# An encoder step on one core: four places where a low part, or the order of two input tiles, changes

## The chip, the core and the metric

The kernel runs on one core of one Trainium2 chip. The metric is the time of one execution on the device, in microseconds (us). The core has five engines that run their own instruction streams and wait for each other through semaphores: TensorE (PE in the profile; its weight loads are PEld), VectorE (DVE), ScalarE (ACT), GpSimd (POOL) and SyncE (SP). SP and POOL issue nearly all of the transfers here.

## The reference

One layer of a streaming encoder over 576 tokens (512 of a prompt and 64 of a running stream), model width 1024, feed-forward width 2816, all in float32:

```
x += 0.5 * SwiGLU_1(RMSNorm(x))
h  = RMSNorm(x); p = h @ w_in                       # 1024 x 7168
y_a = (B_a * dwconv3(C_a * V_a)) @ w_a_out
y_b = swish(LN(dwconv31(GLU(U_b)) + bias)) @ w_b_out
x += (sigmoid(g_a) * y_a + sigmoid(g_b) * y_b) @ w_out
x += 0.5 * SwiGLU_2(RMSNorm(x))
y  = RMSNorm(x)
```

SwiGLU is `(silu(x @ gate) * (x @ up)) @ down`. The outputs are y and the last input rows of the two convolutions.

## The kernel before, in words

Activations lie with features on the 128 partitions and the 576 tokens along the free dimension, so each of the 8 tiles of x is 128x576. Every product is made of matmuls of a 128x128 weight tile with half of the tokens (288 columns).

**Three matmuls for one.** A float32 operand v is split in two parts, hi (v rounded to TensorE's fast float32 form) and lo = v - hi. A product is the sum of hi·hi, hi·lo and lo·hi, and `SIX` lists those three for the two token halves: six matmuls for each weight tile and input tile (line 55 on). The first four entries use the weight's hi, the last two its lo.

**Making a weight's two parts.** The class `Stream` brings weights in: SP loads a raw tile (`load`), ACT rounds it to hi (`begin`), and lo is made in one of two ways. With `"dma"`, ACT writes -hi into the place of lo, and then a transfer that POOL issues adds the raw tile to it. With `"dve"`, VectorE subtracts hi from the raw tile (`end`). There are six raw tiles; a raw tile is free again when the last reader of it is done, which is the adding transfer in the first way and the subtraction in the second. The weights come in units of up to four 128x128 tiles, in an order fixed by a plan that is written before the program; `get` hands out a unit, and `lead` starts units some places ahead. The lo parts (and hi) live in the tiles called `u`, `g` or `act`.

**Products.** `product` makes one output tile (8 input tiles, 48 matmuls where both halves have 4 weight tiles). With `late`, its last two input tiles are taken in turn by `turned`: hi matmuls of the one, all six of the other, then the lo matmuls of the first. `both` makes two output tiles side by side. Where the layout allows, two weight tiles are multiplied by a scheme with seven products of 12 matmuls instead of eight (`plan_block`, `pair`, `block_pair`); its seven weight operands are three plain blocks (a11, a12, a22, which take the way given by `low`) and four sums.

**The stages that the change touches.**
- The head: while x and the first weights still arrive, `multiply(k)` feeds three products (up 0, gate 0, gate 1 of the first feed-forward) with input tile k, k from 0 to 7; `begin(k)` makes the two parts of x's tile k, `split_piece` those of the weights. Then comes the product ("f1", "u", 1), inside of which the total for RMSNorm is formed (`root`).
- The w_out stage: after the last scheme of seven products of w_b_out (`block_pair(3)`), `both` starts the output tiles 0 and 4 of w_out (`IN_TURN` is 0, 4, 1, 5, ...), each of two units.
- The second feed-forward: tile 0 goes by plain products (`PLAIN["f2"]` is 1), tiles 1, 2, ... by `pair`, seven products each.

Instructions go to each engine in the order in which this program is written; nothing is reordered afterwards.

Of the kernel before, what the change touches and what calls it, by code (L numbers as in the profile page):

```python
# [15 lines left out]
P = 128  # L16
D = 1024
KT = D // P
# [4 lines left out]
KU = KT // 2  # L23
# [30 lines left out]
PLAIN = {"f1": 4, "f2": 1}  # L54

IN_TURN = (0, 4, 1, 5, 2, 6, 3, 7)


SIX = ((0, 0), (1, 0), (0, 1), (1, 1), (2, 0), (2, 1))


SHIFT = 32
# [49 lines left out]
def tile_encoder_step(  # L112
# [7 lines left out]
    pe, dve, sca, pool = (  # L120
        Ordered(tc, e, c)
        for e, c in (
            (nc.tensor, pe_cost), (nc.vector, dve_cost), (nc.scalar, None), (nc.gpsimd, None)
        )
    )
# [33 lines left out]
    def psum2():  # L159
        return mmps.tile([P, 2, 512], F32, tag="mm", name=nm("mm"))  # L160
# [161 lines left out]
    homes = [0]  # L322

    def home(other):

        homes[0] += 1
        return ("u", other)[homes[0] % 2]

    def plan_tile(name, w, row0, ks, col0, other, home_of=None, low="dma"):
        plan[name] = []  # L330
        for k in ks:
            r = ws.raw(w, row0, k, col0)
            to = next(home_of) if isinstance(home_of, Iterator) else home_of or home(other)
            plan[name].append(ws.unit(r, k, to, low))
            row0 += k * P

    FIRST = [("f1", "u", 0), ("f1", "g", 0), ("f1", "g", 1)]

    def gu_col(part, i):
        return i * P + (DFF if part == "u" else 0)  # L340

    def plan_pair(f, gu, i):

        plan_block((f, "s", i), [
            ws.raw(gu, h * KU * P, KU, gu_col(part, i)) for part in "ug" for h in range(2)
        ], [home("g") for _ in range(7)], "dve" if (f, i) == ("f1", PLAIN[f]) else "dma")

    def plan_block(name, raws, homes, low="dma"):  # L350

        a21, a22, a11, a12 = raws
        s1, s2, s3, s4 = ((name, n) for n in range(1, 5))
        plan[name] = [
            ws.unit(src, KU, home, how, sums)
            for home, (src, how, sums) in zip(homes, (
                (a11, low, ((s1, (a21, a22)),)),
                (s2, "dve", ((s2, (s1, a11)),)),
                (s1, "dve", ()),
                (s3, "dve", ((s3, (a11, a21)),)),  # L360
                (a12, low, ()),
                (s4, "dve", ((s4, (s2, a12)),)),
                (a22, low, ()),
            ))
        ]
        ws.second.update(plan[name][n] for n in (1, 5, 6))

    def plan_ffn(f, gu, dn):
        for g, grp in enumerate(GROUPS):
            for i in grp:  # L370
                if i >= PLAIN[f]:
                    plan_pair(f, gu, i)
                    continue
                for part in "gu":
                    if (f, part, i) not in plan:
                        plan_tile(
                            (f, part, i), gu, 0, (KU, KU), gu_col(part, i), "g",
                            low="dve" if f == "f1" and (part, i) != ("u", 1) else "dma",
                        )
            n = len(grp)  # L380
            for j in range(KT):
                late = f == "f2" and grp[-1] == FT - 1 and j in LATE
                soon = (f, g) == ("f1", 0) and j < 2 or late and j >= KT - 2
                plan_tile(
                    (f, "d", g, j), dn, grp[0] * P, (n - n // 2, n // 2), j * P, "g",
                    "act" if late else None, "dve" if soon else "dma",
                )
# [27 lines left out]
    for i in range(KU):  # L415
        pair = 2 * i, 2 * i + 1
        if i % 2 == 0:
            for j in pair:

                plan_mixer(("yb", j), w_b_out, j * P, homes_b, "dve")  # L420
        else:

            plan_block(("yb", "s", i), [
                ws.raw(w_b_out, h * P, KU, j * P, 2) for j in pair[::-1] for h in range(2)
            ], [next(homes_b) for _ in range(7)])
    for j in IN_TURN:
        plan_tile(("o", j), w_out, 0, (KU, KU), j * P, "g")
    plan_ffn("f2", ffn2_gu, ffn2_dn)


    def mm(ps, w, kk, xs, first, last, spans=HALVES, six=SIX):


        (whi, wlo), (xh, xl) = w, xs
        parts = ((whi, xh), (whi, xl), (wlo, xh))
        for n, s in six:
            if s < len(spans):
                (a, b), (i, e) = parts[n], spans[s]
                pe.matmul(
                    ps[:, s, : e - i], a[:, kk, :], b[:, i:e],  # L440
                    start=first and n == 0, stop=last and n == 2,
                )

    def chunks(name):

        got = []
        for n in plan[name]:
            w = ws.get(n)
            got += [(w, kk) for kk in range(ws.units[n][1])]
        return got  # L450
# [15 lines left out]
    def fill():  # L466
        while work and dve.time < pe.time - AHEAD:
            work.pop(0)()

    def take():  # L470

        while behind:
            ready, then = behind.pop(0)
            dve.time = max(dve.time, ready)
            then()
# [5 lines left out]
    def turned(p, w, kk, xs, k, last):  # L481

        mm(p, w, kk, xs[k], k == 0, False, six=SIX[:4])
        mm(p, w, kk + 1, xs[k + 1], False, False)
        mm(p, w, kk, xs[k], False, last, six=SIX[4:])

    def product(name, xs, then=None, order=None, got=None, soon=None, late=False):


        if name in early:  # L490
            return early.pop(name)[:, :, :H]
        ps = psum2()
        if order:
            got = chunks(name)
            for n, k in enumerate(order):
                mm(ps, *got[k], xs[k], n == 0, n == len(xs) - 1)
        else:
            at = {0} if turning[0] else set()
            if late:
                at.add(len(xs) - 2)  # L500
            turning[0] = False
            k = 0
            for n in plan[name]:
                w = None
                if not got:
                    w = ws.get(n)
                end = k + ws.units[n][1]
                k0 = k
                while k < end:
                    w = got[k][0] if got else w  # L510
                    if k in at:
                        turned(ps, w, k - k0, xs, k, k + 2 == len(xs))
                        k += 2
                        continue
                    mm(ps, w, k - k0, xs[k], k == 0, k == len(xs) - 1)
                    k += 1
                    if soon and k == 1:
                        soon()
        take()
        if then is None:  # L520
            dve.time = max(dve.time, pe.time)
            return ps[:, :, :H]
        fill()
        behind.append((pe.time, lambda: then(ps[:, :, :H])))

    def both(names, xs, turn=False):
# [4 lines left out]
        for k in range(len(xs)):  # L531
            if turn and k == 1:
                for n, six in (0, SIX[:4]), (1, SIX), (0, SIX[4:]):
                    mm(ps[n], *ws_[n][k], xs[k], False, False, six=six)
# [168 lines left out]
    xg = []  # L703
# [37 lines left out]
    def piece_of(k):  # L741

        for n, size in enumerate(FIRST_KS):
            if k < size:
                return n, k
            k -= size

    first = {name: psum2() for name in FIRST}

    def multiply(k, names=FIRST):  # L750
        n, kk = piece_of(k)
        up, gates = pieces[n][2]

        for six in (SIX,) if k > 0 else (((0, 0), (2, 0), (0, 1), (2, 1)), ((1, 0), (1, 1))):
            for name, (hi, lo), c in zip(FIRST, (up, gates, gates), (0, 0, P)):
                if name in names:
                    w = hi[:, :, c : c + P], lo[:, :, c : c + P]
                    mm(first[name], w, kk, xg[k], k == 0, k == KT - 1, six=six)

    load(0)  # L760
    load_piece(FIRST_KS[0], (nc.sync, sca))
# [15 lines left out]
    begin(1)  # L777
    split_piece(1, sca)
    multiply(0)
    begin(2)  # L780
    split_piece(2, sca)
    multiply(1)
    ss.square(X[0])
    begin(3)
    ss.square(X[1])
    multiply(2)
    begin(4)
    ss.add(dve)
# [36 lines left out]

    ws.ahead = 2
    name = ("f1", "u", 1)
    ps = product(name, xg, soon=root)
    early[name] = ps

    def update(j, ps, R=None):
# [149 lines left out]
    ss, xg = nss, nxg  # L981
# [69 lines left out]
    gates = {}  # L1051
# [32 lines left out]
    xg = xn  # L1084
# [223 lines left out]
    xg = [None] * KT  # L1308
    forms = Forms(R_N2)
    ss = Sum()  # L1310
    xg = [None] * KT
# [3 lines left out]
    for n, j in enumerate(IN_TURN):  # L1315
        ps = two[j] if j in two else product(("o", j), MS)
# [146 lines left out]
```

## Time and profile before

| | |
|---|---|
| median of 3 runs | 1287.59 us (1286.79, 1287.59, 1296.06) |
| the profiled execution | 1297.4 us, its span 1295.4 us |
| PE busy | 1284.4 us (99%), 9728 matmuls |
| DVE, ACT, POOL busy | 924.8, 764.6, 361.1 us (71%, 59%, 28%) |
| granted TensorE clock | 0.998 of full speed, mean |
| transfers issued by POOL | 56160 packets, 92.43 MB, 43.3% of the 16 DMA engines' span |
| transfers issued by SP and ACT | 228784 and 1744 packets, 120.35 and 0.83 MB |

All operations of the compute engines carry one line number (88 before, 92 after), that of a helper that records them, so the trace is read by the names of tiles. Rows of the timeline give the start, the time from the first start to the last end of the rows merged into one, the engine, the operation with its tiles, the count, and in brackets how long the engine had been idle and what ended that. Ends of matmuls are modelled; their starts are recorded, so the steps here go by starts.

### The profile page before, as it was taken

How to read it: one execution, taken by the hardware profiler on the slowest of the kernel's cores; microseconds unless marked ns; L12 is line 12 of the kernel's file. 1: busy time of each engine (PE TensorE's matmuls, PEld its weight loads, DVE VectorE, ACT ScalarE, POOL GpSimd, SP SyncE). 2: the span in 40 equal slices, each digit the busy share in tenths (PEclk: the TensorE clock that was granted, in tenths of full speed). 3: DMA queues.
4: the chain of work that ended last, by engine and by line, in shares of the span. 5: the costliest groups of instructions: out<-in, count | busy, mean ns of one | idle time of the engine just before them, and what ended most of it. 6: DMA issues, size and time to landing. Idle time of an engine off the chain costs nothing.

```text
span 1295.4 us, 25702 instructions
## 1 busy us (share of the span) xinstructions
PE 1284.4 (99%) x9728; PEld 1282.8 (99%) x9728; DVE 924.8 (71%) x1539; ACT 764.6 (59%) x1359; POOL 361.1 (28%) x460
## 2 busy tenths in 40 slices
PE   9999999999999999999999999999999999999997
PEld 9999999999999999999999999999999999999997
DVE  6858668748846998888885166746867858846955
ACT  7645646646776644554444566468664665664664
POOL 0032332332333444333321221132142241241230
PEclk9999999999999999999999999999999999999999
DMA  8286786886799898878875766597588797796783
GB/s 221 69 180 153 163 179 154 179 177 150 153 223 230 177 199 164 169 166 175 168 167 125 165 137 157 143 238 157 124 170 180 159 191 156 161 199 142 154 180 96
DMA packets 286812, 215.26 MB, mean 166 GB/s; under 512 B 15456, under 2 KB 248928, under 8 KB 286688
## 3 DMA queue, kind: packets, MB, share of 16 engines
q0 software_dynamic: 56160, 92.43, 43.3%
q1 hardware_dynamic: 228784, 120.35, 32.5%
q8 instruction: 77, 1.26, 0.4%
q10 hardware_dynamic: 1744, 0.83, 0.2%
q14 instruction: 47, 0.39, 0.1%
HBM read 116.17 MB, written 4.98 MB: 94 GB/s over the span
## 4 chain that ended last, share of the span: by engine, by line
PE 92%; issue 4%; DVE 2%; DMA 1%; ACT 1%; POOL 0%; DVEq 0%; SPq 0%; POOLq 0%; ACTq 0%
PE mm L88 92%; DVE tmp L88 0%; DMA g<-raw 0%; DMA raw<-in_w_b_out_dram 0%; DVE x L88 0%; DMA u<-raw 0%; DVE g L88 0%; ACT act L88 0%; DMA raw<-in_ffn_w_gate_up_dram 0%; DVE act L88 0%; DVE w L88 0%; POOL u L88 0%; ACT u L88 0%; ACT w L88 0%; ACT g L88 0%
## 5 line engine op out<-in xcount | busy, mean ns | idle before, releaser
L88 PE MATMUL mm<-act,u 128*128 128x288 f32 x4758 | 670.8, 294 | 0.5 <-DMA u<-raw 0.5
L88 PEld LDWEIGHTS mm<-act,u 128*128 128x128 f32 x4758 | 641.6, 188 | 0.7 <-DMA u<-raw 0.7
L88 PE MATMUL mm<-act,g 128*128 128x288 f32 x3030 | 432.9, 294 | 0.8 <-DMA g<-raw 0.8
L88 PEld LDWEIGHTS mm<-act,g 128*128 128x128 f32 x3030 | 410.4, 188 | 1.0 <-DMA g<-raw 1.0
L88 POOL DMA_DIRECT2D u<-raw x197 | 171.9, 873 | 487.7 <-ACT u L88 318.8
L88 PE MATMUL mm<-act,act 128*128 128x288 f32 (+2 forms) x1896 | 262.1, 295 | 0.0
L88 PEld LDWEIGHTS mm<-act,act 128*128 128x128 f32 x1896 | 254.5, 189 | 0.3 <-ACT act L88 0.3
L88 ACT CAST u<-raw 128x512 fp32r<-128x512 f32 (+2 forms) x207 | 118.8, 574 | 178.4 <-PE mm L88 145.3
L88 POOL DMA_DIRECT2D g<-raw x126 | 110.0, 873 | 298.4 <-ACT g L88 247.3
L88 DVE SCALAR_TENSOR_TENSOR w<-g,prm,w 128x606 f32<-128x606 f32 x232 | 179.2, 842 | 1.4 <-ACT w L88 1.4
L88 DVE TENSOR_TENSOR tmp<-mm,tmp 128x288 f32<-128x288 f32 (+1 forms) x251 | 112.6, 458 | 71.7 <-PE mm L88 54.9
L88 ACT ACTIVATE u<-u 128x512 fp32r<-128x512 f32 (+2 forms) x197 | 116.8, 593 | 6.2
L88 ACT CAST g<-raw 128x512 fp32r<-128x512 f32 (+2 forms) x136 | 75.1, 552 | 43.0 <-PE mm L88 21.0
L88 DVE SCALAR_TENSOR_TENSOR tmp<-mm,r 128x576 f32<-128x576 f32 x48 | 36.3, 756 | 76.7 <-PE mm L88 76.7
L88 POOL DMA_DIRECT2D act<-raw x67 | 59.2, 883 | 108.9 <-ACT act L88 95.0
L88 ACT CAST act<-tmp 128x576 fp32r<-128x576 f32 x92 | 61.8, 674 | 42.4 <-DVE tmp L88 40.9
L88 ACT CAST u<-w 128x512 fp32r<-128x512 f32 x81 | 50.2, 620 | 62.0 <-DVE w L88 44.1
L88 ACT CAST g<-w 128x512 fp32r<-128x512 f32 x79 | 48.9, 619 | 63.4 <-DVE w L88 56.4
L88 DVE TENSOR_TENSOR act<-tmp,act 128x576 fp32r<-128x576 f32 x92 | 67.5, 753 | 18.1 <-ACT act L88 16.5
L88 ACT ACTIVATE g<-g 128x512 fp32r<-128x512 f32 (+2 forms) x126 | 72.1, 572 | 4.0
L88 DVE TENSOR_TENSOR w<-raw,raw 128x512 f32<-128x512 f32 x82 | 56.1, 685 | 15.1 <-DMA raw<-in_ffn_w_gate_up_dram 11.1
L88 ACT ACTIVATE tmp<-tmp 128x576 f32<-128x576 f32 x47 | 32.2, 685 | 45.9 <-DVE tmp L88 45.9
(86 smaller groups left out, 829.3 us busy)
## 6 DMA issues: line engine op xcount, KB each, us to landing
raw<-in_ffn_w_gate_up_dram SPq DMA_DIRECT2D x171, 256.0 KB, 3.5
u<-raw POOLq DMA_DIRECT2D x140, 256.0 KB, 4.0
raw<-in_w_in_dram SPq DMA_DIRECT2D x112, 256.0 KB, 3.7
raw<-in_ffn_w_down_dram SPq DMA_DIRECT2D x96, 192.0 KB, 3.7
g<-raw POOLq DMA_DIRECT2D x69, 256.0 KB, 4.0
act<-raw POOLq DMA_DIRECT2D x61, 256.0 KB, 4.4
g<-raw POOLq DMA_DIRECT2D x43, 192.0 KB, 4.4
u<-raw POOLq DMA_DIRECT2D x41, 192.0 KB, 4.6
```

Of the source, the lines that this page charges most:

```text
L88: return self.tc.keep_in_program_order(fn(*args, **kwargs))
```

## The change

Four places:
- `multiply(6)` no longer runs its three products one after the other with six matmuls each: the up product does its four hi matmuls, gate 0 its six, up its two lo matmuls, gate 1 its six.
- the product ("f1", "u", 1) is called with `late=True`.
- the lo parts of w_out's first four units (output tiles 0 and 4) are made by VectorE instead of by a transfer.
- in the second scheme of seven products of the second feed-forward (tile 2), the lo part of a22, the last of the seven weight operands, is made by VectorE.

```diff
+FIRST_SIX = (((0, 0), (2, 0), (0, 1), (2, 1)), ((1, 0), (1, 1)))
+
+HEAD_TURN = 6
...
-        ], [home("g") for _ in range(7)], "dve" if (f, i) == ("f1", PLAIN[f]) else "dma")
-
-    def plan_block(name, raws, homes, low="dma"):
+        ], [home("g") for _ in range(7)], {
+            ("f1", PLAIN["f1"]): ("dve", "dve", "dve"), ("f2", PLAIN["f2"] + 1): ("dma", "dma", "dve"),
+        }.get((f, i), ("dma", "dma", "dma")))
+
+    def plan_block(name, raws, homes, lows=("dma", "dma", "dma")):
...
     for j in IN_TURN:
-        plan_tile(("o", j), w_out, 0, (KU, KU), j * P, "g")
+        plan_tile(
+            ("o", j), w_out, 0, (KU, KU), j * P, "g",
+            low="dve" if j in IN_TURN[:2] else "dma",
+        )
...
-    def multiply(k, names=FIRST):
+    def multiply(k):
...
+        steps = [(n, SIX) for n in range(len(FIRST))]
+        if k == 0:
+            steps = [(n, six) for six in FIRST_SIX for n in range(len(FIRST))]
+        elif k == HEAD_TURN:
+            steps = [(0, SIX[:4]), (1, SIX), (0, SIX[4:]), (2, SIX)]
+        for n, six in steps:
+            (hi, lo), c = ((up, 0), (gates, 0), (gates, P))[n]
+            w = hi[:, :, c : c + P], lo[:, :, c : c + P]
+            mm(first[FIRST[n]], w, kk, xg[k], k == 0, k == KT - 1, six=six)
...
-    ps = product(name, xg, soon=root)
+    ps = product(name, xg, soon=root, late=True)
```

On VectorE, around the start of the w_out stage, the order before is this. The `act<-w` row and the two `act<-x` rows make lo parts; the rows with `mm` are sums of the seven products.

```order
L88 TENSOR_TENSOR act_10398<-w_10367,act_10397 128x512
L88 TENSOR_TENSOR tmp_10430<-mm_10444,tmp_10430 128x288
L88 TENSOR_TENSOR tmp_10431<-mm_10483,tmp_10430 128x288 x2
L88 TENSOR_TENSOR tmp_10429<-tmp_10431,mm_10483 128x288
L88 TENSOR_TENSOR act_10540<-x_94,act_10538 128x576
L88 TENSOR_TENSOR act_10544<-x_95,act_10542 128x576
L88 TENSOR_TENSOR tmp_10428<-mm_10523,tmp_10430 128x288
```

Now the same place reads as follows.

```order
L92 TENSOR_TENSOR act_10398<-w_10367,act_10397 128x512
L92 TENSOR_TENSOR g_10458<-raw_10229,g_10457 128x512
L92 TENSOR_TENSOR tmp_10430<-mm_10444,tmp_10430 128x288
L92 TENSOR_TENSOR u_10476<-raw_10252,u_10476 128x512
L92 TENSOR_TENSOR tmp_10431<-mm_10478,tmp_10430 128x288
L92 TENSOR_TENSOR g_10496<-raw_10307,g_10495 128x512
L92 TENSOR_TENSOR tmp_10431<-mm_10478,tmp_10430 128x288
L92 TENSOR_TENSOR tmp_10429<-tmp_10431,mm_10478 128x288
L92 TENSOR_TENSOR act_10533<-x_94,act_10531 128x576
L92 TENSOR_TENSOR act_10537<-x_95,act_10535 128x576
L92 TENSOR_TENSOR u_10514<-raw_10438,u_10514 128x512
L92 TENSOR_TENSOR tmp_10428<-mm_10516,tmp_10430 128x288
```

Four subtractions of a raw tile (into `g` and `u`, the four units of w_out) have come in between the sums. Four steps of ACT that wrote -hi and four transfers of POOL are gone from their engines' streams.

On VectorE, in the second scheme of the second feed-forward, the rows before are these.

```order
L88 TENSOR_TENSOR w_11529<-raw_11386,raw_11388 128x512
L88 TENSOR_TENSOR tmp_11375<-mm_11508,tmp_11373 128x288
L88 TENSOR_TENSOR w_11554<-w_11529,raw_11449 128x512
L88 TENSOR_TENSOR tmp_11375<-tmp_11375,tmp_11374 128x576
L88 TENSOR_TENSOR tmp_11524<-mm_11561,tmp_11524 128x288
```

Now they are these.

```order
L92 TENSOR_TENSOR w_11525<-raw_11382,raw_11384 128x512
L92 TENSOR_TENSOR tmp_11371<-mm_11504,tmp_11369 128x288
L92 TENSOR_TENSOR u_11527<-raw_11097,u_11527 128x512
L92 TENSOR_TENSOR w_11549<-w_11525,raw_11445 128x512
L92 TENSOR_TENSOR tmp_11371<-tmp_11371,tmp_11370 128x576
L92 TENSOR_TENSOR tmp_11520<-mm_11556,tmp_11520 128x288
```

One subtraction (`u<-raw`, a22's lo) has come in behind the last sum of the scheme before it.

On PE, in the head, input tile 6 (`act_297` and `act_298` are its hi and lo; 302 and 303 those of the up weights, 306 and 307 those of the two gates) reads so before.

```order
L88 MATMUL mm_108<-act_297,act_302 128x288
L88 MATMUL mm_108<-act_298,act_302 128x288
L88 MATMUL mm_108<-act_297,act_302 128x288
L88 MATMUL mm_108<-act_298,act_302 128x288
L88 MATMUL mm_108<-act_297,act_303 128x288 x2
L88 MATMUL mm_109<-act_297,act_306 128x288
L88 MATMUL mm_109<-act_298,act_306 128x288
L88 MATMUL mm_109<-act_297,act_306 128x288
L88 MATMUL mm_109<-act_298,act_306 128x288
L88 MATMUL mm_109<-act_297,act_307 128x288 x2
```

Now it reads so.

```order
L92 MATMUL mm_108<-act_297,act_302 128x288
L92 MATMUL mm_108<-act_298,act_302 128x288
L92 MATMUL mm_108<-act_297,act_302 128x288
L92 MATMUL mm_108<-act_298,act_302 128x288
L92 MATMUL mm_109<-act_297,act_306 128x288
L92 MATMUL mm_109<-act_298,act_306 128x288
L92 MATMUL mm_109<-act_297,act_306 128x288
L92 MATMUL mm_109<-act_298,act_306 128x288
L92 MATMUL mm_109<-act_297,act_307 128x288 x2
L92 MATMUL mm_108<-act_297,act_303 128x288 x2
```

The two matmuls with the up weights' lo have moved from the fifth and sixth place to the eleventh and twelfth; their number is the same.

More of the change, by code (lines that the diff above doesn't have):

```diff
@@ L356, in plan_block @@
             for home, (src, how, sums) in zip(homes, (
-                (a11, low, ((s1, (a21, a22)),)),
+                (a11, lows[0], ((s1, (a21, a22)),)),
                 (s2, "dve", ((s2, (s1, a11)),)),
@@ L360, in plan_block @@
                 (s3, "dve", ((s3, (a11, a21)),)),
-                (a12, low, ()),
+                (a12, lows[1], ()),
                 (s4, "dve", ((s4, (s2, a12)),)),
-                (a22, low, ()),
+                (a22, lows[2], ()),
             ))
@@ L748, in tile_encoder_step @@
     first = {name: psum2() for name in FIRST}
-    def multiply(k, names=FIRST):
+    def multiply(k):
         n, kk = piece_of(k)
         up, gates = pieces[n][2]
[L754 to L758, printed above, removed]
+        steps = [(n, SIX) for n in range(len(FIRST))]
[7 more added lines that the diff above has]
+            mm(first[FIRST[n]], w, kk, xg[k], k == 0, k == KT - 1, six=six)
     load(0)
```

## The prediction

> **What bounds the kernel now.** I read the page first, then PE's waits, then PE's timeline where a wait stands, then the engines that feed PE there. On the page:
>
> ```profile
> span 1295.4 us, 25702 instructions
> PE 1284.4 (99%) x9728; PEld 1282.8 (99%) x9728; DVE 924.8 (71%) x1539; ACT 764.6 (59%) x1359; POOL 361.1 (28%) x460
> ```
>
> PE runs nearly without a break, so only its number of matmuls, their pitch, and its few waits set the end. The change keeps the number. The waits of PE for transfers, in all (engine, whom it waited for, total us, times, longest):
>
> ```profile
> PE mm L88 <- DMA g<-raw: 0.8, 1, 0.8
> PE mm L88 <- DMA u<-raw: 0.5, 1, 0.5
> ```
>
> Each happened once. The bracketed figures use modelled ends; I size the two losses by starts. PE around the w_out stage (start, length, operation, count; two answers of the timeline):
>
> ```profile
> 832.28 3.32 PE L88 MATMUL mm<-act,u 128*128 128x288 f32 x24
> 835.44 3.33 PE L88 MATMUL mm<-act,g 128*128 128x288 f32 x24
> 838.61 1.74 PE L88 MATMUL mm<-act,u 128*128 128x288 f32 x12
> ```
>
> ```profile
> 848.11 3.10 PE L88 MATMUL mm<-act,g 128*128 128x288 f32 x22
> 851.99 5.27 PE L88 MATMUL mm<-act,g 128*128 128x288 f32 x38 [0.77 <-DMA g<-raw]
> 857.10 6.48 PE L88 MATMUL mm<-act,u 128*128 128x288 f32 x48
> ```
>
> Undisturbed, 24 matmuls take 835.44 - 832.28 = 3.16 us, a pitch of 0.1317. From 848.11 to 857.10 there are 22 + 38 = 60 matmuls, 7.90 us at that pitch, in 8.99: **1.09 us lost**. The row of 22 is 12 of the last product of `block_pair(3)` and 10 of the w_out stage: six of output tile 0, four with the hi of tile 4's first unit. What is waited for is that unit's lo.
>
> PE in the second feed-forward:
>
> ```profile
> 925.52 1.75 PE L88 MATMUL mm<-act,u 128*128 128x288 f32 x12
> ...
> 933.45 1.75 PE L88 MATMUL mm<-act,g 128*128 128x288 f32 x12
> 935.03 0.43 PE L88 MATMUL mm<-act,u 128*128 128x288 f32 x2
> 935.92 1.58 PE L88 MATMUL mm<-act,u 128*128 128x288 f32 x10 [0.46 <-DMA u<-raw]
> 937.34 1.75 PE L88 MATMUL mm<-act,g 128*128 128x288 f32 x12
> ```
>
> A product of 12 takes 935.03 - 933.45 = 1.58 us; the one from 935.03 took 2.31: **0.73 us lost**. A scheme is seven products; the one that begins at 925.52 is the second, and its seventh, a22's, is the one that waits.
>
> **The w_out units.** Who is late there (ACT, then DVE, then POOL):
>
> ```profile
> 845.01 0.62 ACT L88 CAST g<-raw 128x512 fp32r<-128x512 f32 x1 [1.45 <-PE mm L88]
> ```
>
> ```profile
> 845.14 0.82 DVE L88 TENSOR_TENSOR tmp<-mm,tmp 128x288 f32<-128x288 f32 x2 [2.28 <-PE mm L88]
> 848.06 1.43 DVE L88 TENSOR_TENSOR act<-x,act 128x576 fp32r<-128x576 f32 x2 [1.61 <-ACT act L88]
> ```
>
> ```profile
> 846.59 0.86 POOL L88 DMA_DIRECT2D g<-raw  x1 [1.88 <-ACT g L88]
> ```
>
> The same transfer's group of issues (KB each, us to landing):
>
> ```profile
> g<-raw POOLq DMA_DIRECT2D x1, 256.0 KB, 5.4
> ```
>
> Hi ends at 845.63, the adding transfer is issued at 846.59 and lands 5.4 us later, at 851.99, when PE goes on. After the change VectorE subtracts as soon as hi is there. I price a subtraction by its nearest row, a DVE subtraction of the same shape:
>
> ```profile
> 837.36 0.69 DVE L88 TENSOR_TENSOR g<-w,g 128x512 fp32r<-128x512 f32 x1
> ```
>
> So this lo is ready near 845.63 + 0.69 = 846.3, four and a half us before PE asks (848.11 + 22 x 0.132 = 851.0). The wait goes whole: **-1.09**. The four subtractions, 2.8 us, fall into DVE's idle 2.28 and 1.61 us, and the four ACT steps and four POOL issues that go free those engines. Behind the subtraction that waits for hi stand on DVE the second sum of the row at 845.14 (from about 845.6 to 846.3), a difference and the two lo parts of x (848.06 before, bound by ACT, which is now earlier). PE needs those two from input tile 4, 48 matmuls into the stage, about 856: cover of over 6 us. If that cover were gone, each subtraction would cost its 0.69. A raw tile that comes free sooner lets SP load sooner; see the last rival.
>
> **The a22 unit.** ACT, DVE, and POOL with the issue groups of its transfers:
>
> ```profile
> 929.58 0.60 ACT L88 CAST u<-raw 128x512 fp32r<-128x512 f32 x1
> 930.22 0.63 ACT L88 ACTIVATE u<-u 128x512 fp32r<-128x512 f32 x1
> ```
>
> ```profile
> 930.08 0.45 DVE L88 TENSOR_TENSOR tmp<-mm,tmp 128x288 f32<-128x288 f32 x1
> 930.45 0.68 DVE L88 TENSOR_TENSOR w<-w,raw 128x512 f32<-128x512 f32 x1
> 932.34 0.46 DVE L88 TENSOR_TENSOR tmp<-mm,tmp 128x288 f32<-128x288 f32 x1 [0.55 <-ACT tmp L88]
> ```
>
> ```profile
> 921.84 0.86 POOL L88 DMA_DIRECT2D u<-raw  x1 [4.18 <-ACT tmp L88]
> ...
> 931.81 0.86 POOL L88 DMA_DIRECT2D u<-raw  x1 [4.36 <-ACT g L88]
> 932.35 1.21 POOL L88 DMA_DIRECT2D g<-raw  x1
> ...
> 942.79 0.86 POOL L88 DMA_DIRECT2D u<-raw  x1 [0.32 <-ACT tmp L88]
> ```
>
> ```profile
> u<-raw POOLq DMA_DIRECT2D x1, 256.0 KB, 4.1
> g<-raw POOLq DMA_DIRECT2D x1, 256.0 KB, 4.8
> ```
>
> The wait is on 931.81 + 4.1 = 935.9. VectorE would have this lo at 930.53 + 0.69 = 931.2. **-0.73.** On DVE the added 0.69 pushes w (930.45) and what follows; the idle 0.55 takes most of it. The weight sum that is pushed (930.45) feeds the next scheme's second product, after 938.9: cover of 6 us. ACT saves 0.63 us just before the next unit's hi.
>
> **What is late next.** PE comes 1.09 earlier to all that lies behind 852, and 1.82 earlier behind 936. Up to the second wait the feeding chain starts from the w_out products themselves, so it moves along: the u transfer of 921.84, landing 3.5 us on (row below) at 925.34, is needed by the third matmul at 925.52 + 0.26 = 925.78 and keeps its 0.44. Behind the second wait the 0.73 is not shared by all of the chain. The g transfer of 932.35 lands at 937.15 and is needed at 937.60: 0.45 to spare. It gains the 0.63 of ACT and a queue without its predecessor, so I take it as just enough. The u transfer of 942.79 is similar:
>
> ```profile
> u<-raw POOLq DMA_DIRECT2D x1, 256.0 KB, 3.5
> ```
>
> ```profile
> 948.44 1.75 PE L88 MATMUL mm<-act,u 128*128 128x288 f32 x12
> ```
>
> ```profile
> u<-raw POOLq DMA_DIRECT2D x1, 256.0 KB, 4.9
> ```
>
> Landing 947.69, needed 948.70: 1.0 to spare, less 0.73, less up to 0.3 by which DVE is later. New waits here lie between 0 and the whole 0.73; I take 0.3, since the spare of each is near the gain and the spread of landings (3.5 to 5.4 in these rows) is larger than what remains.
>
> **The head and its next product.** The rows:
>
> ```profile
> 24.93 0.95 PE L88 MATMUL mm<-act,g 128*128 128x288 f32 x6
> ```
>
> ```profile
> 17.66 1.02 DVE L88 TENSOR_TENSOR act<-g,act 128x256 fp32r<-128x256 f32 x2
> ```
>
> Input tile 6 begins 36 matmuls before 24.93, at 20.2. Its weights' lo parts, which the moved matmuls read, end on DVE at 18.68. So nothing waits: moving lo matmuls back six places gains 0, bringing gate 0's lo forward by two costs 0. A gain would need PE 1.5 us earlier. `late=True` moves the last lo matmuls of a product in the same way; a product ordered so (835.44, 3.17 us to the next start) takes what the plain one before it takes (3.16). 0.
>
> **Sum.** -1.09 - 0.73 + 0.3 + 0 = -1.5 us. The profiled execution goes from 1297.4 to 1295.9. That execution is 9.8 us above the median of the runs shown, 1287.59, and near the one run of 1296.06. The waits are a few tenths of a per cent at most, so I carry the difference over: 1287.59 - 1.5 = **1286.1 us**.
>
> **Rivals.**
> *The transfers behind set the pace* (0.17): waits return at the transfers with 0.4 to 1.0 to spare, and 0.2 to 1.0 of the 1.82 stays, or the two waits belong to this one execution and the timed runs have little of them. 1287.0. For it: the spare times; against: the chain moves with PE.
>
> *VectorE holds up POOL* (0.04). POOL's issue at 932.35 took 1.21 instead of the usual 0.86 us; DVE was busy just then. If each added subtraction holds a POOL issue by 0.35 (these rows) to 0.69, a whole subtraction, the g transfer with 0.45 to spare is late by that less its spare, and the sum is -1.5 + 0.2 = -1.3: 1286.3. Against: the DVE row at 837.36 is of the same kind, and POOL's issue beside it took the usual time:
>
> ```profile
> 837.52 0.86 POOL L88 DMA_DIRECT2D u<-raw  x1 [10.16 <-DVE x L88]
> ```
>
> The Trainium skill, SBUF — State Buffer, section "SBUF: two separate sides", has a rule that speaks against this change: a VectorE operation with two SBUF inputs and a GpSimd operation that reads SBUF exclude each other for the whole instruction. By it each added subtraction could hold POOL for 0.69 us; the row of 837.52 does not agree, that of 932.35 might.
>
> *Slower: earlier loads collide with the next transfer* (0.06). A raw tile that VectorE has read is free four us sooner. SP's load waited for just that:
>
> ```profile
> 935.96 0.37 SPq L239 DMA_DIRECT2D raw<-in_ffn_w_gate_up_dram  x1
> ```
>
> It would start near 931.2 and run beside the g transfer of 932.35, whose 4.8 us could become 7.0, as the slowest of the w_out stage did:
>
> ```profile
> g<-raw POOLq DMA_DIRECT2D x1, 256.0 KB, 7.0
> ```
>
> Landing 939.35 against a need at 937.60 - 1.82 = 935.78 is a wait of 3.6 for 1.82 gained: +1.8, 1289.4. It decides from a landing after 937.60 on. Against: that transfer itself starts earlier.
>
> *The long execution* (0.20): one of three runs, and the profiled one, are 8 to 10 us longer than the others, and I find no wait in the trace that makes it. If two of three runs are so, the median is 1296.06 - 1.5 = 1294.6, with the change as forecast.
>
> **How the numbers follow.** The forecast has 0.53, and its own range is 1287.59 - 1.82 - 1.6 (twice the 0.8 between the two short runs, for another set of runs) to 1287.59 - 1.1 + 1.6: 1284.2 to 1288.1. The cases of 1287.0, 1286.3 and 1289.4 end close to it; the long execution's 1294.6, with 0.9 for its scatter, takes the range to 1295.5. Left out are gains larger than any wait shown, and runs longer than the longest so far. A measurement of this kernel can tell about 1%, 12.9 us; every case above is inside it, so within 1% gets 0.97, faster 0.01, slower 0.02.
>
> **What would show it.** In the profile after: no PE wait on g<-raw near 851 or on u<-raw near 935; the product from 935.03 takes 1.58; POOL has five DMA issues fewer, ACT five steps fewer, DVE five subtractions of 0.69 more; the head's rows stand where they stood. Wrong would be a new PE wait between 920 and 950 that is longer than 0.3, or a PE wait on DVE.

## The result, and the profile after

Changed kernel: 1297.24 us (median of 22 runs, 1293.35 to 1298.31). Kernel before, measured beside it: 1291.16 us (22 runs, 1286.79 to 1299.39). The ratio is 1.0032, 95% interval 1.0016 to 1.0048: slower, by well under the 1% that the chances go by. The forecast was 1286.1, within 1284.2 to 1295.5. The profiled execution went from 1297.4 to 1298.2 us.

The times of a kernel here lie in two clusters, about 1286 to 1292 and 1293 to 1299. Of the 22 runs of before 12 lie in the lower one, of the changed kernel none. A run under 1292.5 is called a **low run** from here on. The clock does not part the clusters: in the runs of the experiments the mean granted clock is 0.996 to 0.999, with a median of 0.998 in the low runs and in the others.

The page after, and PE's waits:

```profile
span 1296.3 us, 25688 instructions
PE 1286.3 (99%) x9728; PEld 1285.0 (99%) x9728; DVE 928.7 (72%) x1544; ACT 761.8 (59%) x1354; POOL 357.2 (28%) x455
```

```profile
PE mm L92 <- POOL eps L92: 1.0, 1, 1.0
PE mm L92 <- ACT tmp L92: 0.5, 1, 0.5
```

Both waits for transfers are gone; these two stand at the start and the end, in before too. DVE has five instructions more, ACT and POOL five fewer. The two places (two excerpts of PE's timeline):

```profile
848.01 8.09 PE L92 MATMUL mm<-act,g 128*128 128x288 f32 x60
855.93 6.48 PE L92 MATMUL mm<-act,u 128*128 128x288 f32 x48
```

```profile
933.87 1.75 PE L92 MATMUL mm<-act,u 128*128 128x288 f32 x12
935.45 1.75 PE L92 MATMUL mm<-act,g 128*128 128x288 f32 x12
```

The 60 matmuls take 7.92 us instead of 8.99 (-1.07); a22's product, from 933.87, takes 1.58 where it took 2.31 (-0.73). The subtractions that did it, on DVE:

```profile
845.56 0.69 DVE L92 TENSOR_TENSOR g<-raw,g 128x512 fp32r<-128x512 f32 x1
```

```profile
929.29 0.68 DVE L92 TENSOR_TENSOR u<-raw,u 128x512 fp32r<-128x512 f32 x1
```

So far all is as forecast: behind a22 PE stands at 935.45 where it stood at 937.34, 1.89 us ahead. The end is later all the same, and no wait takes the gain back. PE's timeline just behind, in before and in after:

```profile
959.54 4.91 PE L88 MATMUL mm<-act,g 128*128 128x288 f32 x36
964.29 3.28 PE L88 MATMUL mm<-act,u 128*128 128x288 f32 x24
967.41 2.50 PE L88 MATMUL mm<-act,g 128*128 128x288 f32 x18
```

```profile
957.65 5.17 PE L92 MATMUL mm<-act,g 128*128 128x288 f32 x36
962.66 3.32 PE L92 MATMUL mm<-act,u 128*128 128x288 f32 x24
965.82 2.54 PE L92 MATMUL mm<-act,g 128*128 128x288 f32 x18
```

Look at the steps from start to start. In before 24 matmuls take 967.41 - 964.29 = 3.12 us, in after 965.82 - 962.66 = 3.16: the same instructions with another **pace**, 130.0 against 131.7 ns each. Of the 1.89 us by which after leads, 0.26 goes in the row of 36 (964.29 - 962.66 is 1.63), most of it in a small wait: two steps near 959 are 0.18 us too long together. The rest, and more, goes up to the end. From 962 to 1270 before fits 16 more matmuls into the same time:

```profile
962.00:1140.00 178.00, 178.00 (x1360) 1.00 0.78 168
1140.00:1270.00 130.00, 130.00 (x991) 1.00 0.80 168
```

```profile
962.00:1140.00 178.00, 178.00 (x1351) 1.00 0.79 167
1140.00:1270.00 130.00, 130.00 (x984) 1.00 0.79 167
```

The columns are the stretch, its length, PE's busy time, its matmuls in brackets, the granted clock, the DMA engines' share and GB/s (before first, then after). 16 x 0.131 = 2.1 us, at a granted clock of 1.00 and an equal load of transfers in both. PE is "busy" for the whole of each stretch, so its share of 99% shows nothing of this.

That accounts for most of the difference between the two profiled executions: after's last matmul starts 0.55 us later, and the other 0.35 of the 0.9 us of span lies behind it. It does not yet account for 22 runs without a low one; the experiments do.

### The profile page after: what moved, and what is told of

Same layout as the page of the kernel before. It is cut to its first block, busy times and chain, and to the rows that moved or that the text cites. A ratio compares the mean times of both kernels' runs of the same rounds, so it can differ in the third digit from the quotient of the medians.

```text
span 1296.3 us, 25688 instructions
## 1 busy us (share of the span) xinstructions
PE 1286.3 (99%) x9728; PEld 1285.0 (99%) x9728; DVE 928.7 (72%) x1544; ACT 761.8 (59%) x1354; POOL 357.2 (28%) x455
## 4 chain that ended last, share of the span: by engine, by line
PE 99%; DVE 0%; ACT 0%; DVEq 0%; issue 0%; POOL 0%; POOLq 0%
PE mm L92 99%; DVE g L92 0%; DVE tmp L92 0%; DVEq L1466 0%; DVE r L92 0%; DVE x L92 0%; ACT tmp L92 0%; ACT r L92 0%; POOL tmp L92 0%; POOL eps L92 0%; POOLq L1457 0%
```

## The experiments

Each kernel ran 12 times. "Low" gives its low runs; kernels measured together (e1 to e4, e5 to e8, e9 to e12, e13 to e15) share the runs of before. Before had 79 low runs of 156 in all, the 22 above included. Diffs are against the changed kernel unless another one is named.

| kernel | median us | low | ratio to before |
|---|---|---|---|
| five subtractions alone (e1) | 1288.49 | 10 of 12 | 0.9971 [0.9946, 0.9997] |
| changed, no `late` (e2) | 1297.25 | 4 | 1.0014 [0.9986, 1.0042] |
| changed, no turn in the head (e3) | 1297.52 | 0 | 1.0028 [1.0004, 1.0052] |
| before with `late` alone (e4) | 1296.69 | 0 | 1.0029 [1.0006, 1.0052] |
| before with the head's turn alone (e8) | 1297.01 | 1 | 1.0027 [1.0004, 1.0050] |
| e1, four more units by DVE (e5) | 1296.37 | 4 | 1.0000 [0.9971, 1.0030] |
| e5, total asked for sooner (e6) | 1296.84 | 2 | 1.0021 [0.9996, 1.0045] |
| e6, other order in the total (e7) | 1296.08 | 2 | 1.0021 [0.9997, 1.0045] |
| e5, two more units by DVE (e9) | 1287.61 | 7 | 0.9975 [0.9942, 1.0009] |
| e9, a wait in the total (e10) | 1298.16 | 2 | 1.0018 [0.9990, 1.0046] |
| e10, other order in the total (e11) | 1298.08 | 0 | 1.0041 [1.0017, 1.0064] |
| e1, `late` one product on (e12) | 1296.56 | 0 | 1.0020 [0.9997, 1.0044] |
| e1, `late` far from the head (e13) | 1296.39 | 0 | 1.0037 [1.0016, 1.0058] |
| e1, a turn at a product's start (e14) | 1297.36 | 0 | 1.0048 [1.0028, 1.0068] |
| e3, a second turn behind `late` (e15) | 1289.11 | 8 | 0.9993 [0.9964, 1.0022] |

**Which part of the change does it (e1 to e4, e8).** e1 leaves both reorderings out, e2 and e3 one each; e4 and e8 are before with one each.

```diff
-HEAD_TURN = 6
+HEAD_TURN = None                                # e1, e3, e4
-    ps = product(name, xg, soon=root, late=True)
+    ps = product(name, xg, soon=root)            # e1, e2, e8
-            low="dve" if j in IN_TURN[:2] else "dma",
+            low="dma",                           # e4, e8
-            ("f2", PLAIN["f2"] + 1): ("dma", "dma", "dve"),          # e4, e8
```

> Only the five subtractions by VectorE; the head and the product behind the total are ordered as before. Theory A (TensorE has two paces, 1580 and 1560 ns for 12 plain matmuls, which hold until something disturbs them; the order of the head's end decides which one holds for the first 800 us): times in two clusters as before, near 1286 and near 1295, each up to 1.8 us under that of before, no PE wait near 850 and 935. Theory B (the subtractions themselves, or the loads that they bring forward, cost the time): nearly all runs at 1296 to 1298, as the whole change.

> The whole change without late=True on the product behind the total. Theory A, with late as the step that takes TensorE out of the short pace: the short pace that the trace after shows for the first 30 matmuls or so of that product stays, 1560 ns for 12 plain matmuls from 27 us on, and most runs come out at 1284 to 1288, below both kernels. Theory B: 1296 to 1298, since the subtractions are still there. Theory C (the turn at input tile 6 decides, not late): 1296 to 1298 as well.

> The whole change without the turn at input tile 6. Theory A with late as the cause: 1296 to 1298 in nearly all runs, 1580 ns for 12 plain matmuls. Theory C (the turn is the cause): two clusters as before, median under 1292. Theory B: 1296 to 1298.

> Kernel before with late=True on the product behind the total and nothing else. Theory A with late as the cause: nearly all runs at 1296 to 1300 (the long pace, with up to 1.8 us of waits that are still there). Theories B and C: two clusters as before, median near 1291.

> Kernel before with the turn at input tile 6 and nothing else. If the turn changes only which runs get the short pace: two clusters as before, near 1288 and 1297, their shares anywhere. If the turn itself costs the pace as late does: nearly all at 1296 to 1299. If it did nothing: 18 of 35 runs in the lower cluster, as the kernel before.

The five subtractions alone come out faster than before, 0.9971. Much of that is their 10 low runs of 12 against before's 18 of 35, and a share can fall so by chance: e5 and e9, with the same head, have 4 and 7. The median of e1's low runs, 1287.64, is 1.95 us under that of before's beside it, 1289.59. The sign and size fit the forecast gain, but before's low runs alone have medians from 1288.18 to 1289.59 in its five sets of runs, so 1.95 is good to one or two us. Every kernel with `late` on that product has no low run. Where a reader can see why is PE's timeline just behind the head. A product of 48 matmuls is two rows of 24 here. The second half of ("f1", "u", 1), with the turn at its end, is the row at 28.70 in after; the total's six matmuls are ahead of the first row shown. After, then before, then e1, then e4:

```profile
28.70 3.29 PE L92 MATMUL mm<-act,u 128*128 128x288 f32 x24
31.83 3.32 PE L92 MATMUL mm<-act,g 128*128 128x288 f32 x24
34.99 3.32 PE L92 MATMUL mm<-act,u 128*128 128x288 f32 x24
```

```profile
28.76 3.33 PE L88 MATMUL mm<-act,u 128*128 128x288 f32 x24
31.92 3.33 PE L88 MATMUL mm<-act,g 128*128 128x288 f32 x24
```

```profile
27.97 3.28 PE L92 MATMUL mm<-act,u 128*128 128x288 f32 x24
31.09 3.28 PE L92 MATMUL mm<-act,g 128*128 128x288 f32 x24
34.21 3.28 PE L92 MATMUL mm<-act,u 128*128 128x288 f32 x24
```

```profile
28.07 3.29 PE L92 MATMUL mm<-act,u 128*128 128x288 f32 x24
31.20 3.32 PE L92 MATMUL mm<-act,g 128*128 128x288 f32 x24
34.36 3.32 PE L92 MATMUL mm<-act,u 128*128 128x288 f32 x24
```

Before's profiled execution has 3.16 from the start. e1 has 3.12 throughout. After and e4 begin short (3.13 with the turn in it) and have 3.16 from the next product on; e3 does the same, and e2, which has no turn there, came out of the head in the long pace and stays in it. So both paces come out of the head, and the turn ends the short one. What that is worth over the kernel, after against e1:

```profile
24.00:260.00 236.00, 236.00 (x1791) 1.00 0.71 152
260.00:400.00 140.00, 140.00 (x1064) 1.00 0.84 181
400.00:800.00 400.00, 400.00 (x3041) 1.00 0.80 169
800.00:948.00 148.00, 148.00 (x1124) 1.00 0.66 153
```

```profile
24.00:260.00 236.00, 236.00 (x1805) 1.00 0.72 153
260.00:400.00 140.00, 140.00 (x1072) 1.00 0.85 186
400.00:800.00 400.00, 400.00 (x3079) 1.00 0.80 169
800.00:948.00 148.00, 148.00 (x1134) 1.00 0.70 156
```

e1 fits in 14 + 8 + 38 + 10 = 70 more matmuls by 948, 70 x 0.131 = 9.2 us. The rest of the 9.9 us between the two spans (1296.3 and 1286.4) is that e1's product began 0.73 us sooner in its execution. This is the distance between the two clusters.

The head's turn seems to take low runs away too: 5 of 24 without `late` (e2, e8), against 21 of 36 for the kernels with neither (e1, e5, e9). e2 was expected to have mostly low runs and has 4. No trace shows how; the count is all there is, and e1, e5 and e9 differ among themselves by 10, 7 and 4.

In the long pace the subtractions gain nothing that can be seen: e3, which has them, takes 1297.52, and e4, which has not, 1296.69. e4's profiled execution changes to 3.12 behind 962, as before's does; e3's does not.

**More gain of the same kind (e5, e9).** PE's last small waits in the second feed-forward, met by more subtractions: the four lo parts of two output tiles of the down product (e5), and those of a11 in two schemes (e9).

```diff
-                soon = (f, g) == ("f1", 0) and j < 2 or late and j >= KT - 2
+                soon = g == 0 and j < 2 or late and j >= KT - 2      # e5, on e1
...
-            ("f2", PLAIN["f2"] + 1): ("dma", "dma", "dve"),
+            ("f2", PLAIN["f2"] + 1): ("dve", "dma", "dve"),         # e9, on e5
+            ("f2", PLAIN["f2"] + 2): ("dve", "dma", "dma"),
```

> The five subtractions of the change, the head as before, and VectorE also makes the four lo parts of the first two output tiles of the second feed-forward's first down product, where the runs without the two waits all lose the short pace at a small wait near 959 us. Theory A: that wait is gone, a run that has the short pace keeps it to the end (1560 ns for 12 plain matmuls behind 962 too); the lower cluster moves from 1286 to 1290 down to 1283 to 1288, the upper one stays at 1296 to 1298, and the share of the lower one is about half, as before. Rival (the short pace ends there for another reason, as the step from the scheme of seven products to plain ones): no change against the five subtractions alone.

> The five subtractions and those of the down product, the head as before, and VectorE also makes the lo parts of a11 in the second and third scheme of the second feed-forward, for which TensorE waited 0.1 to 1 us in the traces so far once it came earlier. Theory A: no gap over 0.2 us between 900 and 970 us; a run that has the short pace from 27 us on keeps it to the end and takes 1282 to 1286; the upper cluster stays at 1296 to 1298. Rival (the pace is lost at the step from one kind of product to the other): the lower cluster stays at 1285 to 1289.

e5's profiled execution has no wait where e1's had one near 949, and yet 3.16 from 952.57 on, so its expectation failed: that wait is not all that ends the short pace there. In e9's profile the short pace holds to the end (span 1284.0), with no gap in PE up to 1260 us, and its low runs' median, 1285.93, is 3.0 us under that of before's beside it (1288.96). But five of its twelve runs stand at 1297.19 to 1297.48, where before's upper cluster lies too: the tuning of waits moved the lower cluster and not the upper one, and it did not decide which of them a run falls in. e9's gain as a whole is not told from none.

**Is it a wait in the head that picks the pace (e6, e7, e10, e11)?** The total is asked for ahead of the product, and the parts that it sums are made late (`later` additional sums that nothing reads).

```diff
+    root()
+    ps = product(name, xg)                          # in place of soon=root
-    ss.gather()
+    ss.gather(later=2)                              # e6, e7 half a tile each; 3 whole ones in e10, e11
-                for s, out in enumerate(room):
-                    for one, v in self.terms:
+                for one, v in self.terms:
+                    for s, out in enumerate(room):  # e7, e11
```

> As the run before, and the total for RMSNorm is multiplied ahead of the product behind it, with two small additions that serve nothing ahead of its lo part, so that TensorE must wait for it: after the first of the six matmuls of the total. Theory A, with the pace set by the state in which TensorE restarts after a wait: the runs are no longer in two clusters, all are in the short or all in the long pace (1284 to 1289, or 1296 to 1298), the wait itself costing up to 1 us. If the pace is drawn anew at every run, two clusters stay.

> As the run before, with the total's three hi matmuls ahead of the three of lo, so that the wait comes after three matmuls and three follow. Theory A with a set restart: one cluster again, perhaps the other one. If the restart doesn't set the pace: two clusters, the same shares as in the run before.

> As the run before, and the total multiplied ahead of the product behind it, with three small additions that serve nothing ahead of its lo part, so that TensorE waits 1 to 2 us for it after the first of the total's six matmuls. If the restart after a wait sets the pace: one cluster, at 1284 to 1288 or at 1297 to 1300. If not: two clusters.

> As the run before with the total's three hi matmuls first, so that the wait comes after three and three follow. If the restart sets the pace: one cluster, the same or the other one. If not: two clusters.

In e6 and e7 the sums were ready in time and PE did not wait, so those two say nothing on a wait; they show what the total ahead of the product does without one, 4 low runs of 24. In e10 PE did wait:

```profile
24.42 0.25 PE L92 MATMUL mm<-tmp,ones_r 128*128 128x192 f32 x1
25.65 0.80 PE L92 MATMUL mm<-tmp,ones_r 128*128 128x192 f32 x5 [0.99 <-DVE tmp L92]
26.29 3.35 PE L92 MATMUL mm<-act,g 128*128 128x288 f32 x24
29.48 3.32 PE L92 MATMUL mm<-act,u 128*128 128x288 f32 x24
32.64 3.32 PE L92 MATMUL mm<-act,g 128*128 128x288 f32 x24
```

3.16 behind it, and 2 low runs of 12; with a shorter wait behind the third matmul (e11) none. So a wait there does not bring the short pace. That it makes the long one likely is not shown, since 2 of 24 with the wait is not told from the 4 of 24 without it.

A wait elsewhere may do the opposite. Eleven of the profiled executions come to 900 us in the long pace. Six of them waited 0.2 us or more between 923 and 936 (before, e4 and e8 for a22; e12, e13 and e14, which have the subtractions, for other transfers), and just these six have 3.12 behind 962. In before the short pattern does not begin at the wait, though, but some 25 us later, in the row of 36 at 959.54, right behind a turn that the kernel already had there (`both` with `turn`). So the wait and the turn may both be needed; no run parts them.

**Is it the place, or the turn (e12 to e15)?** e12 moves `late` one product on, e13 puts it on a product near 85 us with plain products on both sides, e14 turns the first two tiles of the product ("f1", "g", 2), and e15 has `late` as in the change and that turn right behind it.

```diff
-            ups = product(up, xg, got=got, late=f == "f1" and i == PLAIN[f] - 1)
+            ups = product(up, xg, got=got, late=f == "f1" and i >= PLAIN[f] - 2)     # e12, on e1
-   update(j, product((f, "d", g, j), hs, late=j == KT - 1), R)
+   update(j, product((f, "d", g, j), hs, late=j == KT - 1 or (f, g, j) == ("f1", 0, 4)), R)   # e13, on e1
+            turning[0] = (f, i) == ("f1", 2)        # ahead of the gate product; e14 on e1, e15 on e3
             ps = product((f, "g", i), xg, order=IN_TURN if f == "f2" and i == 0 else None)
```

> The five subtractions with the head as before, and the turn of the last two input tiles put on the product ('f1', 'u', 2), two products behind the one where the change has it. If a turn at the end of a plain product between two plain products always costs the short pace: nearly all runs at 1296 to 1298, as with late=True on ('f1', 'u', 1). If only that one place does it: two clusters, near 1287 and 1297.

> The kernel with the five subtractions alone, with the last two tiles of one product taken in turn: output tile 4 of the first feed-forward's first down part, near 85 us, far from the head, with plain products ahead of it and behind it. Two paces, ended by any turn ahead of a plain product: where the head gives the short pace (24 matmuls in 3.12 us), it holds to about 85 us and is 3.16 from the next product on; no run under 1292, median 1296 to 1297.5. Two paces, but only the head is open to it: as with the five subtractions alone, most runs at 1286 to 1290, 3.12 on both sides of the turn, which itself costs 0.01 to 0.05 us. Third case: 3.16 behind the turn, and 3.12 again behind the next stretch of seven-product schemes: low runs some 0.1 to 1 us above those of the five subtractions alone.

> The five subtractions alone, with the first two tiles of the product of gate tile 2 taken in turn (near 31 us), so the turn stands at the start of a plain product and not at its end. If any turn between plain products ends the short pace: 3.16 behind it, no run under 1292, median 1296 to 1297.5. If only a turn at a product's end does: 3.12 behind it, runs spread as with the five subtractions alone (more than half at 1286 to 1290).

> The changed kernel without the turn of the head's products, with the turn of the last two tiles of up tile 1 kept and a turn of the first two tiles of the next product (gate tile 2) right behind it. If the pace is a phase that one turn shifts and the next can shift back: 3.12 behind both, some runs at 1286 to 1290. If a turn between plain products only ever ends the short pace: no run under 1292, median 1296.5 to 1298 as with the one turn alone.

PE's timeline of e12 and of e13 around the turn, which is in the second row of each:

```profile
37.20 3.28 PE L92 MATMUL mm<-act,g 128*128 128x288 f32 x24
40.32 3.29 PE L92 MATMUL mm<-act,u 128*128 128x288 f32 x24
43.45 3.32 PE L92 MATMUL mm<-act,g 128*128 128x288 f32 x24
46.61 3.32 PE L92 MATMUL mm<-act,u 128*128 128x288 f32 x24
```

```profile
83.07 2.50 PE L92 MATMUL mm<-act,u 128*128 128x288 f32 x18
85.41 1.73 PE L92 MATMUL mm<-act,g 128*128 128x288 f32 x12
86.98 2.54 PE L92 MATMUL mm<-act,u 128*128 128x288 f32 x18
89.35 1.75 PE L92 MATMUL mm<-act,g 128*128 128x288 f32 x12
```

In e12 the row at 40.32 holds the turn: 3.12 ahead of it, 3.16 from 43.45 on. In e13 it is the row at 85.41: 18 matmuls take 2.34 us ahead of it and 2.37 behind it. So it is the turn and not its place, and neither kernel has a low run. e14 has none either, but its profiled execution came out of the head in the long pace and keeps it: its turn, in the row from 31.20, leaves 3.16 as it was. And e15, the change's own turn with a second one behind it:

```profile
28.57 3.29 PE L92 MATMUL mm<-act,u 128*128 128x288 f32 x24
31.70 3.31 PE L92 MATMUL mm<-act,g 128*128 128x288 f32 x24
34.85 3.28 PE L92 MATMUL mm<-act,u 128*128 128x288 f32 x24
37.97 3.28 PE L92 MATMUL mm<-act,g 128*128 128x288 f32 x24
```

3.13, 3.15, and 3.12 again, with 8 low runs of 12 where the one turn has none. That is the first of the two answers written down for it: the pace behaves like a **phase** of the stream that one turn shifts and the next can shift back. The second turn was seen to do so only right behind the first; the same turn left e14's long pace alone. It also fits that the turns that the kernel already had leave the short pace as it is in e1 (70 matmuls more by 948): most of them stand at the end of a product ahead of a seven-product scheme, and behind that scheme the next plain products begin with a turn. That last point is read from the code and the two profiles; no run took such a pair apart.

## Why the prediction was wrong

**Right, term by term.** The w_out wait: -1.09 forecast, -1.07 measured. The a22 wait: -0.73 forecast, -0.73 measured. The two subtractions were forecast ready at 846.3 and 931.2 and ended at 846.25 and 929.97. The cover held: no PE wait on DVE. All the signs named for the profile after are there, five instructions each way and the product of 1.58 among them. In low runs, e1 is 1.95 us under before, which fits the two terms within the scatter named above.

**The term of new waits**, +0.3: 0.26 near 958 in the profiled execution, 0.18 of it wait, and none at the two transfers that were named. The one with 0.45 us to spare, the g transfer of 932.35, was on time in after, but is what PE waits for near 935 in the profiled executions of e12 (0.4 us) and e13 (1.1). The term was sized fairly; it varies from one execution to the next.

**Wrong: "a product ordered so (835.44, 3.17 us to the next start) takes what the plain one before it takes (3.16). 0."** This is the step that failed. Both rows were taken from a stretch in the long pace, where a turn has nothing to end. In the short pace it costs 0.01 us in its own product (3.13) and some 0.04 in every 24 plain matmuls behind it, 9.2 us by 948. The forecast priced the turn as so many instructions at one duration; its cost lies in the instructions that follow. The head's turn, priced 0 by the same reasoning, seems to cost low runs too.

The a22 wait was sized rightly and still gave little in the long pace: in the profiled executions in the long pace that no longer wait there or near it (after, e2, e3, e10, e11) the change to 3.12 behind 962 is missing too, which is 2.1 us between before and after for the 0.73 gained. The forecast took the pace behind the wait as fixed.

**Wrong: "The long execution", 0.20, with "the change as forecast".** The clusters were treated as scatter that the change leaves alone. The text did look for a wait and found none, which is right; the cause is no wait. It was to be seen in the one trace at hand: before's own rows, 3.16 at 832.28 and 3.12 at 964.29, hold both paces. Stretched over 1290 us, 0.04 in 3.16 is 16 us, room enough for the 8 to 10 us that the text leaves without a cause. With that, the case of 1294.6 would have needed a condition: what sets the pace, and whether a reordering behind the head touches it. That its time lies within 3 us of the measured 1297.24 is luck; its reason, two long runs of three drawn by chance, is not what happened.

**The other rivals.** "VectorE holds up POOL" misread its row. The issue before it, at 931.81, ran until 931.81 + 0.86 = 932.67, and from there the issue of 932.35 took 0.89 us, near the usual 0.86. The other issues of before that start while one is under way do the same, so the 1.21 was a place in the queue, not DVE. In after, where that predecessor is gone, it takes its usual time, and beside DVE's work:

```profile
930.51 0.86 POOL L92 DMA_DIRECT2D g<-raw  x1 [4.21 <-ACT tmp L92]
```

"Earlier loads collide": a wait of some 3.6 us near 936 was its sign, and after has none there. SP's load did come sooner, at 930.00 for 935.96, but the g transfer beside it landed 4.9 us after its issue, against 4.8 before; e13's wait of 1.1 is the longest seen at that transfer. "Transfers behind set the pace" is the term above. Slower came out, but by a mechanism that no rival had.

What stays open is why the short pace falls to about half of the runs of before, and how the stream inside PE keeps a phase. The turns show that order moves the share; e6, e7, e10 and e11, all with the total ahead of the product, have 6 low runs of 48, but what in them does it was not parted. Neither says what the state is.

## What to carry to other kernels

Where TensorE is busy nearly without a break, read its pace from start to start in every stage, not its busy share: here the same matmuls ran at two paces, and 1% of pace outweighed every wait that was left. A reordering inside such a stream that costs nothing by count has to be weighed by the pace of what follows it, and it takes a dozen runs or more, since one execution shows one draw of it. Where the times of a kernel fall into two clusters, find what parts them before pricing a change of a microsecond; the change without its two reorderings (e1) is the version to keep here, and what it gains by its two waits shows in the low runs only.

## What the runs showed that was not expected

PE has two steady paces for the same stream at a granted clock of 1.00: 24 plain matmuls in 3.12 or 3.16 us. In the record of single starts the short one repeats every six matmuls (the six of one weight and input tile), 780 ns, and the long one every twelve, 1580 ns. Steps between starts in ns, in e1 from 29.0 us, in before from 30.1 and in e15 around its two turns:

```
e1:     131 133 130 126 129 131 | 131 133 130 126 129 131 | ...
before: 133 132 132 131 130 131 134 132 131 133 128 133 | 133 132 132 131 130 131 134 132 131 133 128 ...
e15, both turns: ... 133 130 128 133 136 126 131 129 131 129 132 133 133 132 136 136 137 134 134 130 | 126 128 132 131 133 130 | 126 128 ...
```

Each pace, once there, goes on for hundreds of microseconds (e1 and before from about 30 to 900). The Trainium skill, TensorE: Matmul & The Clock Gate, section "Back-to-back issue gap", says that in a stream of weight loads and matmuls the spacing is set by both together; that leaves room for what is seen, but it gives one spacing for a size, and here one size has two.
